# Feed-forward of a hybrid decoder layer: seven block products in the place of eight (2x2x2 blocks)

## The chip, the core and the metric

The kernel runs on one NeuronCore of a Trainium2 chip. The metric is device time in microseconds (us) of one execution. The engines that matter here are TensorE (PE in the profile; PEld is its weight load), VectorE (DVE), ScalarE (ACT), GpSimd (POOL) and SyncE (SP), whose queue issues the loads from memory. [...]

## What is computed

One layer for 544 tokens: 512 of a prompt and 8 x 4 of running sequences. The change touches the two products of the feed-forward alone:

```python
def layer_norm(x, g, b):
...
    mix = (jax.nn.sigmoid(g_a) * y_a + jax.nn.sigmoid(g_b) * y_b) @ w_out
    x1 = layer_norm(DN_ALPHA * x + mix, ln1_g, ln1_b)
    ff = jnp.square(jax.nn.relu(x1 @ w_ff1)) @ w_ff2
    ple = jax.nn.sigmoid(x1 @ w_ple_gate) * (p @ w_ple_proj)
    y = layer_norm(DN_ALPHA * x1 + ff + ple, ln2_g, ln2_b)
```

`x1` is 544 x 1024, `w_ff1` 1024 x 4096 and `w_ff2` 4096 x 1024, all in float32.

## The kernel before

Activations lie with the channels on the 128 partitions and the 544 tokens along a row, so a weight tile is 128 x 128 and a column tile of a product is 128 output channels by 544 tokens. The tokens are worked on in two runs of columns, 256 and 288 (`HALVES`), which lie in two PSUM banks of one buffer.

Every product of float32 numbers is made of three: each operand is split into a high part, rounded by a ScalarE copy to the type that TensorE reads (`hi`, `x1h`, `hid_0h`), and a low part, the VectorE difference of the operand and its high part (`lo`, `x1l`, `hid_0l`); the three passes of `mm` are high weight by high activation, high by low, and low by high. Each weight tile thus costs three passes over 544 columns.

Weights come as a stream of chunks (128 x 1024 numbers, 512 KB). `stream` loads a chunk into one of three `raw` buffers by SP's queue, ScalarE makes `hi`, VectorE makes `lo`, a few chunks ahead of TensorE. `pair` takes two column tiles of a product: two chunks for 1024 input channels, two PSUM buffers of the ring `mm` (three buffers of two banks each, `mm_psum`), and an evacuation function for each column tile when its sum is complete. While one tile is evacuated, TensorE works on the next in another buffer.

The feed-forward goes in quarters of the 4096 hidden channels, in the order of `ff_order`: stage (1, q) makes quarter q of the hidden layer, where ScalarE applies ReLU and the square and VectorE makes the low part (`evac_ff1`), and stage (2, q) multiplies that quarter by its part of `w_ff2` and VectorE adds the result from PSUM to the eight accumulators `acc` (`evac_ff2`). The last stage, (2, 3), runs with `by_halves`: all column tiles for the first run of tokens and then for the second, so that the second layer norm can begin (`between3`). Before the feed-forward stand the first layer norm and the per-layer gate (`evac_ple`), which set `x1` and the first value of `acc`.

The order in which an engine's instructions stand is set by `fill` and the class `Clocks`: work beside the products waits in sequences (`put`), and is issued where the planner's estimate of the engine's time falls behind its estimate for TensorE, or when its due chunk comes (`need`). All instructions go through one helper, so they all have one line in the profile (line 137) and are told apart by the tiles they read and write.

Of the kernel before, what the change touches and what calls it, by code (L numbers as in the profile page):

```python
# [9 lines left out]
F32 = mybir.dt.float32  # L10
# [5 lines left out]
P = 128  # L16
# [7 lines left out]
# the 544 token columns lie in two PSUM banks, as 256 + 288 neighbouring columns  # L24
# [3 lines left out]
SLOTS = 71  # L28
# [12 lines left out]
LN1_PRIO = 0.1  # L41
STREAM_PRIO = 0.15
# [19 lines left out]

def tname(x):
    return x.tensor.name
# [9 lines left out]
class Clocks:  # L74
    """estimates of when each engine comes to its work, from which the order of issue follows"""
# [35 lines left out]
    def op(self, e, name, out, args, kw):  # L111
# [4 lines left out]
        if e == "D":  # L116
# [25 lines left out]
def tile_hybrid_step(ctx: ExitStack, tc: tile.TileContext, I, O):  # L142
# [35 lines left out]
    # ---------------------------------------------------------------- constants  # L178
# [11 lines left out]
    # TensorE has its full clock only after a stretch of work: begin that while the first loads are under way  # L190
# [5 lines left out]
    # ---------------------------------------------------------------- weight stream  # L196
# [15 lines left out]

    raws, his, splits, held, fast, stacked = {}, {}, {}, set(), set(), set()
# [11 lines left out]
    def parts(j, tag):  # L225
        """a chunk's split weights: one buffer, or two of the activations' for a chunk that is held for long"""
# [34 lines left out]
    def split_first(a, b):  # L261
        """columns a to b of the first chunk, which comes in pieces"""
# [16 lines left out]
    def stream(e, i):  # L279
        """the next load, high or low part of a weight that engine e may take up beside chunk i"""  # L280
# [70 lines left out]
    def fill():  # L351
        horizon = clocks.t["T"] + LEAD
        moved = True
        while moved:
            moved = False
            for e in "DSVGT":
                while clocks.t[e] < horizon:
                    now = clocks.t[e]
                    it = stream(e, state["next"] - 1)
# [23 lines left out]
    # ---------------------------------------------------------------- products  # L383
# [13 lines left out]
    def pair(acts, mt0, evac, nkt=None):  # L397
        """two 128-column tiles of a product; its chunks come next in the stream"""
# [13 lines left out]
    def by_halves(acts, mt0, nmt, evac, between=None):  # L412
        """column tiles, all of the first token half before the second"""
# [21 lines left out]
    def split_later(prio, src, name, done_, due, *deps):  # L435
        """the two parts of an activation as a sequence of its own"""
# [18 lines left out]
    # ---------------------------------------------------------------- stream order  # L455
# [32 lines left out]
    ff_order = [(1, 0), (1, 1), (2, 0), (1, 2), (2, 1), (1, 3), (2, 2), (2, 3)]  # L488
    for kind, q in ff_order:
        if kind == 1:  # L490
            plan(I["w_ff1"][0], D, 1024 * q, 4)
        else:
            for p in range(4):
                for r in range(2):
                    w_spec(I["w_ff2"][0], 1024 * q + 512 * r, 4, 256 * p, 256)
    held.update(range(len(specs) - 4, len(specs)))

    # ---------------------------------------------------------------- x, feature-major
# [27 lines left out]
    # ---------------------------------------------------------------- parameters and states  # L526
# [37 lines left out]
    def param_math():  # L564
        # softplus(-lam) = max(-lam, 0) + 2 atanh(e / (2 + e)), e = exp(-|lam|)
# [19 lines left out]
        # c2 * r is half of -log(a)  # L585
# [3 lines left out]
    # ---------------------------------------------------------------- layer norms  # L589
    class Norm:  # L590
        """mean and variance over the 1024 channels of eight feature-major tiles, per token half"""
# [52 lines left out]
        def put(self, h, prio, due, after, *deps):  # L644
            """queue the steps up to 1 / deviation, and then after()"""
# [101 lines left out]
    # ---------------------------------------------------------------- branch b  # L747
# [519 lines left out]
```

## Time and profile before

| what | value |
|---|---|
| median of 3 runs | 1005.63 us (1005.08 to 1007.27) |
| span of the profiled execution, first to last instruction | 1004.8 us |
| mean granted TensorE clock, whole span | 0.984 |
| loads and stores | 97.87 MB, mean 97 GB/s |

The profile gives the profiled execution by its span; that execution has no separate time, and the median of the runs stands 0.8 us above the span. Busy time is the time in which an engine had an instruction in flight; records of neighbouring instructions can overlap, so the step from one start to the next is what an engine is occupied with one, and the duration is how long until its result is there. "x24" in a row of the timeline merges 24 equal instructions.

### The profile page before, as it was taken

Reading aid. Unit: us, or ns where it says so; the run is one execution under the profiler, and the core shown is the slowest. Engines: PE = TensorE matmul, PEld = TensorE weight load, DVE = VectorE, ACT = ScalarE, POOL = GpSimd, SP = SyncE. Lnnn points to the kernel's source line nnn. Section 1 sums busy time; section 2 is a strip of 40 time slices with the busy share of each in tenths; the row PEclk is TensorE's granted clock in tenths of the full one; section 3 lists DMA queues with packets and bytes.
Section 4 is the critical chain, followed back from the end, with each engine's and each line's share of the span. In section 5 each row is a group of like instructions: output and inputs, shape, how many; then the busy total and the mean of one; then the engine's idle time right before and its main releaser. Section 6 shows DMA issues by size and latency. Waiting matters only on the chain.

```text
span 1004.8 us, 17739 instructions
## 1 busy us (share of the span) xinstructions
PE 964.2 (96%) x7560; PEld 959.4 (95%) x7560; DVE 646.2 (64%) x939; ACT 413.1 (41%) x600; POOL 179.6 (18%) x173
## 2 busy tenths in 40 slices
PE   8999979989889997999999999999999999999995
PEld 8999979989889997999999999999999999999995
DVE  5698889897899999794468952323322222233447
ACT  6432428643467321563225834455114511541301
POOL 0342765455332700001200000000000000000002
PEclk9999989999899998999999999999999999999998
DMA  8333324332332222326251402222232332222402
GB/s 291 93 95 103 107 65 155 104 100 61 88 117 73 64 78 91 107 84 197 84 169 43 125 24 84 85 84 85 87 99 73 97 108 84 85 84 85 125 29 84
DMA packets 89279, 97.87 MB, mean 97 GB/s; under 512 B 4208, under 2 KB 82416, under 8 KB 89200
## 3 DMA queue, kind: packets, MB, share of 16 engines
q1 hardware_dynamic: 89200, 96.74, 31.1%
q8 instruction: 59, 0.97, 0.4%
q14 instruction: 20, 0.16, 0.1%
HBM read 89.71 MB, written 3.81 MB: 93 GB/s over the span
## 4 chain that ended last, share of the span: by engine, by line
PE 72%; DVE 12%; POOL 7%; ACT 5%; issue 3%; DMA 1%; SPq 0%; DVEq 0%; ACTq 0%; POOLq 0%
PE ps L137 55%; PE psq L137 14%; DVE ca L137 5%; DVE lo L137 2%; POOL prod L137 2%; POOL cbs L137 2%; POOL ctx_b L137 1%; PE pps L137 1%; ACT th L137 1%; PE rg L137 1%; ACT L137 1%; ACT hi L137 1%; ACT aa L137 1%; DVE s L137 1%; DVE th L137 1%
## 5 line engine op out<-in xcount | busy, mean ns | idle before, releaser
L137 ACT ACTIVATE hi<-raw 128x1024 fp32r<-128x1024 f32 (+4 forms) x177 | 167.7, 957 | 284.1 <-PE ps L137 217.2
L137 DVE TENSOR_TENSOR lo<-raw,hi 128x1024 fp32r<-128x1024 f32 (+3 forms) x173 | 194.4, 1148 | 13.2 <-ACT hi L137 13.0
L137 DVE SCALAR_TENSOR_TENSOR ca<-u,par_a,ca 128x482 f32<-128x482 f32 (+29 forms) x240 | 179.6, 806 | 1.3 <-ACT ca L137 0.9
L137 PE MATMUL ps<-x1l,hi 128*128 128x288 f32 x616 | 128.3, 290 | 0.6 <-DVE x1l L137 0.6
L137 PE MATMUL ps<-x1h,hi 128*128 128x288 f32 x616 | 127.6, 289 | 0.6 <-ACT x1h L137 0.6
L137 PE MATMUL ps<-x1h,lo 128*128 128x288 f32 x616 | 127.6, 288 | 0.0
L137 PEld LDWEIGHTS ps<-x1h,hi 128*128 128x128 f32 x616 | 94.8, 189 | 0.8 <-ACT x1h L137 0.8
L137 PEld LDWEIGHTS ps<-x1l,hi 128*128 128x128 f32 x616 | 94.6, 189 | 0.8 <-DVE x1l L137 0.8
L137 PEld LDWEIGHTS ps<-x1h,lo 128*128 128x128 f32 x616 | 94.9, 189 | 0.0
L137 POOL TENSOR_TENSOR y<-y,rows_g 128x512 f32<-128x512 f32 x2 | 3.1, 1547 | 461.1 <-ACT y L137 461.1
L137 DVE TENSOR_TENSOR acc<-acc,ps 128x544 f32<-128x544 f32 x24 | 17.3, 722 | 93.8 <-PE ps L137 93.8
L137 ACT ACTIVATE ff<-ps 128x544 f32<-128x544 f32 x32 | 20.0, 624 | 51.2 <-PE ps L137 51.2
L137 POOL TENSOR_TENSOR prod<-ctx_a,par_a 128x248 f32<-128x248 f32 x32 | 36.9, 1206 | 0.0
L137 PE MATMUL psq<-x1l,hi 128*128 128x288 f32 (+1 forms) x128 | 36.9, 288 | 0.0
L137 PE MATMUL psq<-x1h,lo 128*128 128x288 f32 (+1 forms) x128 | 36.8, 288 | 0.0
L137 PE MATMUL psq<-x1h,hi 128*128 128x288 f32 (+1 forms) x128 | 36.8, 287 | 0.0
L137 PE MATMUL ps<-x0h,hi 128*128 128x288 f32 x104 | 23.2, 306 | 10.5 <-ACT gate L137 9.0
L137 PEld LDWEIGHTS ps<-x0h,hi 128*128 128x128 f32 x104 | 16.7, 198 | 11.7 <-ACT gate L137 9.7
L137 PE MATMUL ps<-x0h,lo 128*128 128x288 f32 x104 | 22.3, 297 | 5.3 <-DVE lo L137 5.3
L137 ACT ACT_TABLE_LOAD x20 | 25.7, 1283 | 1.4 <-PEq L1257 0.7
L137 POOL COPY ctx_b<-bx 128x32 f32<-128x32 f32 x10 | 21.2, 2125 | 26.6 <-ACT bx L137 26.6
L137 POOL TENSOR_TENSOR sa<-sa,sb 128x544 f32<-128x544 f32 x6 | 10.9, 1812 | 77.3 <-DVE sa L137 77.3
(616 smaller groups left out, 2647.7 us busy)
## 6 DMA issues: line engine op xcount, KB each, us to landing
raw<-in_w_ff_dram SPq DMA_DIRECT2D x64, 512.0 KB, 4.2
raw<-in_w_in_dram SPq DMA_DIRECT2D x51, 512.0 KB, 3.6
xr<-in_x_dram SPq DMA_DIRECT2D x16, 272.0 KB, 5.3
raw<-in_w_proj_b_dram SPq DMA_DIRECT2D x8, 512.0 KB, 3.4
raw<-in_w_proj_a_dram SPq DMA_DIRECT2D x8, 512.0 KB, 4.1
raw<-in_w_out_dram SPq DMA_DIRECT2D x8, 512.0 KB, 3.5
raw<-in_w_ple_gate_dram SPq DMA_DIRECT2D x8, 512.0 KB, 3.9
out_dram<-y SPq DMA_DIRECT2D x8, 256.0 KB, 2.0
```

Source lines behind the costliest of these rows:

```text
L137: return fn(out, *args, **kw)
```

## The change

Both products of the feed-forward are cut into blocks of 256 x 256 weights and of 256 channels by 544 tokens. A block product is a 2 x 2 by 2 x 2 product of 128 x 128 weight tiles (A11, A12, A21, A22) and of activation pieces of 128 channels by 272 tokens (B11, B12, B21, B22), and it is made with seven products of pieces instead of eight. The seven products take the weights A11, S3, S2, A22, S1, A12 and S4 in this order (numbered 1, 7, 6, 4, 5, 2, 3), where S1 = A21 + A22, S3 = A11 + A21, S2 = S3 + A22 and S4 = S2 + A12 are formed by VectorE from the loaded blocks before they are split (`SUMS_BY_DMA = False`), and the activations B11, t3, t2, t4, t1, B21 and B22, where t1 to t4 are differences of the four pieces, formed by VectorE as well: once for `x1` (`plan_x_forms`) and once for each block of the hidden layer (`make_hid`). A "panel" is the seven products for 256 output channels. The four results of a panel are combined from partial sums: alpha (products 1, 6, 5, 3, one after another on top of each other), delta (7, 4) and beta (2). Alpha and beta lie in the two banks of one `mm` buffer, delta in a bank of the ring `misc`. Since alpha goes on growing, each of its intermediate values is read by ScalarE or VectorE before the next product is added to it.

There are 16 panels of 256 hidden channels for `w_ff1`, of which the first is made plainly with eight products (`ff1_four`, which needs no t1 to t4), and for `w_ff2` four groups of three hidden blocks, each with four panels (`ff2_seven`), while the last four hidden blocks are multiplied plainly by halves (`ff2_halves`), as the last quarter was before. The weights are laid out on the host by blocks; a load brings 128 x 512 (w_ff1) or 128 x 384 numbers (w_ff2), 256 or 192 KB, and two of them share a `raw` buffer. A loaded or summed block is a unit with its own place in `raw`, `hi` and `lo`. `SLOTS`, the number of activation buffers, goes from 71 to 72.

```diff
+FORM_AHEAD = {"D": 7, "G": 6, "V": 4, "S": 5}
+HALF = T // 2
+SUMS_BY_DMA = False
...
-    ff_order = [(1, 0), (1, 1), (2, 0), (1, 2), (2, 1), (1, 3), (2, 2), (2, 3)]
...
+    SEVEN = ("A11", "S3", "S2", "A22", "S1", "A12", "S4")
+    FOUR = ("A11", "A12", "A21", "A22")
...
+        else:
+            lo(us["A11"])
+            total(us["S3"], us["S1"], us["A11"])
+            total(us["S2"], us["S3"], us["A22"])
+            lo(us["S3"])
+            total(us["S1"], us["S1"], us["A22"])
+            lo(us["S2"])
+            lo(us["A22"]), lo(us["S1"])
+            total(us["S4"], us["S2"], us["A12"])
+            lo(us["A12"]), lo(us["S4"])
...
+    GROUPS = ((0, 3), (3, 3), (6, 3), (9, 3), (12, 4))
+    stages = []
+    for g, upto in enumerate((4, 7, 10, 14, 16)):
+        start = (0, 4, 7, 10, 14)[g]
+        stages += [(1, p) for p in range(start, upto)] + [(2, g)]
...
+        def t13():
+            a.extend(act(f"xt{q}_{i}") for i in range(2))
+            V.tensor_sub(half(a[0], 0), b11, b12)
+            V.tensor_sub(half(a[0], 1), b22, b12)
+
+        def t24():
+            V.scalar_tensor_tensor(half(a[1], 0), half(a[0], 0), -1.0, b22, op0=OP.mult, op1=OP.subtract)
+            V.scalar_tensor_tensor(half(a[1], 1), half(a[1], 0), -1.0, b21, op0=OP.mult, op1=OP.subtract)
...
+    def mm3(ps, u, k, a, start, stop, more):
+        w = slice(k * P, k * P + P)
+        for pi, (ww, aa) in enumerate(((u.hi, a[0]), (u.hi, a[1]), (u.lo, a[0]))):
+            TE.matmul(ps, ww[:, w], aa, start=start and pi == 0, stop=stop and pi == 2,
+                      skip_group_check=more)
+
+    def seven(fs, name, after):
+
+        ab, d = mm_psum(name), misc_psum(name + "d")
+        al, be, de = ab[:, :HALF], ab[:, 512:512 + HALF], d[:, :HALF]
+        for nm, ps, start, b in ((1, al, True, "B11"), (7, de, True, "t3"), (6, al, False, "t2"), (4, de, False, "t4"),
+                                 (5, al, False, "t1"), (2, be, True, "B21"), (3, al, False, "B22")):
+            u = take()
+            for k, f in enumerate(fs):
+                mm3(ps, u, k, f()[b], start and k == 0, k == len(fs) - 1, not start)
+                fill()
+            release(u)
+            after(nm, ps)
+            fill()
...
+            elif nm == 4:
+                b["Y"], b["Z"] = act(f"fy{p}"), act(f"fz{p}")
+                c21 = half(b["Z"], 0) if plain else half(b["Y"], 1)
+                V.scalar_tensor_tensor(c21, ps, -1.0, half(b["W"], 0), op0=OP.mult, op1=OP.subtract)
+            elif nm == 5:
+                c22 = half(b["Z"], 1 if plain else 0)
+                V.scalar_tensor_tensor(c22, ps, -1.0, half(b["X"], 1), op0=OP.mult, op1=OP.subtract)
+            elif nm == 2:
+                V.tensor_add(half(b["Y"], 0), ps, half(b["X"], 0))
...
+    def ff2_seven(g):
+        q0, nq = GROUPS[g]
+        for mp in range(4):
+            c = [[half(acc[2 * mp + i], l) for l in range(2)] for i in range(2)]
+
+            def after(nm, ps):
+                out, op = {1: (c[0][0], V.tensor_add), 7: (c[1][1], V.tensor_sub), 6: (c[1][0], V.tensor_sub),
+                           4: (c[1][0], V.tensor_sub), 5: (c[1][1], V.tensor_sub), 2: (c[0][0], V.tensor_add),
+                           3: (c[0][1], V.tensor_add)}[nm]
+                op(out, out, ps)
+            seven([lambda q=q: hid_forms[q] for q in range(q0, q0 + nq)], f"g{g}_{mp}", after)
...
-    for kind, q in ff_order:
+    for kind, n in stages:
         if kind == 1:
-            e = evac_ff1(q)
-            for p in range(4):
-                pair(x1, 2 * p, e)
-        elif q < 3:
-            for p in range(4):
-                pair(hid[q], 2 * p, evac_ff2)
-            hid[q] = None
+            (ff1_seven if n else ff1_four)(n)
+            if n == 15:
+                x1 = x_forms = None
+        elif n < 4:
+            ff2_seven(n)
         else:
-            by_halves(hid[q], 0, 8, evac_ff2, between3)
+            ff2_halves()
```

The order of the instructions moves on every engine. First place, TensorE within a panel of `w_ff2`, before: column tiles of a stage (2, q); `ps` is the PSUM buffer of the tile, `hid` the hidden layer, and two runs of columns follow each other for every pair of operands.

```order
L137 MATMUL ps_0_8888<-hid_4h,hi_8784 128x288
L137 MATMUL ps_0_8888<-hid_4h,hi_8784 128x256
L137 MATMUL ps_0_8888<-hid_4l,hi_8784 128x288
L137 MATMUL ps_0_8888<-hid_4l,hi_8784 128x256
L137 MATMUL ps_0_8888<-hid_4h,lo_8834 128x288
L137 MATMUL ps_0_8888<-hid_4h,lo_8834 128x256
```

The changed kernel at the end of product 5 (weights S1, activation t1, called hh0B), through product 2 (A12, B21, hh0A) to the beginning of product 3 (S4, B22). `g_2_7716` is the buffer that holds both alpha and beta of the third panel of the first group; the words in brackets name the semaphores that an instruction waits for (DVE is VectorE's, Activation ScalarE's).

```order
L149 MATMUL g_2_7716<-hl2B,fhi_7696 128x272
L149 MATMUL g_2_7716<-hh2B,flo_7697 128x272
L149 MATMUL g_2_7716<-hh0A,fhi_7725 128x272 [waits DVE_49,Activation_49]
L149 MATMUL g_2_7716<-hl0A,fhi_7725 128x272
L149 MATMUL g_2_7716<-hh0A,flo_7726 128x272
L149 MATMUL g_2_7716<-hh1A,fhi_7725 128x272
L149 MATMUL g_2_7716<-hl1A,fhi_7725 128x272
L149 MATMUL g_2_7716<-hh1A,flo_7726 128x272
L149 MATMUL g_2_7716<-hh2A,fhi_7725 128x272
L149 MATMUL g_2_7716<-hl2A,fhi_7725 128x272
L149 MATMUL g_2_7716<-hh2A,flo_7726 128x272
L149 MATMUL g_2_7716<-hh0B,fhi_7725 128x272 [waits DVE_49,Activation_49]
```

A sum that was made of one uninterrupted run into its own buffer is now made of products that each begin with a wait for VectorE. In the built program the first of the two values waited for is the one that VectorE reaches with its sum after product 5 (`acc_6263<-acc_6263,g_2_7716`), and the second the one after product 2; beta and alpha are different banks, but one tile to the framework that sets the waits.

Second place, VectorE in the same stretch, before: `acc` is an accumulator, `lo` a low part of the weight stream.

```order
L137 TENSOR_TENSOR acc_6260<-acc_6260,ps_0_8888 128x544
L137 TENSOR_TENSOR acc_6261<-acc_6261,ps_1_8889 128x544
L137 TENSOR_TENSOR lo_9004<-raw_8836,hi_8944 128x1024
L137 TENSOR_TENSOR lo_9058<-raw_8894,hi_9002 128x1024
L137 TENSOR_TENSOR acc_6262<-acc_6262,ps_0_9000 128x544
```

The changed kernel from product 6 of that panel to product 1 of the next: `fraw` are weight blocks and sums (a row `fraw<-fraw` is a sum), `flo` low parts, `g_2d` is delta.

```order
L149 TENSOR_TENSOR acc_6263<-acc_6263,g_2_7716 128x272
L149 TENSOR_TENSOR acc_6263<-acc_6263,g_2d 128x272
L149 TENSOR_TENSOR flo_7769<-fraw_7732,fhi_7768 128x384
L149 TENSOR_TENSOR fraw_7776<-fraw_7732 128x384
L149 TENSOR_TENSOR acc_6263<-acc_6263,g_2_7716 128x272
L149 TENSOR_TENSOR fraw_7790<-fraw_7776 128x384
L149 TENSOR_TENSOR flo_7769<-fraw_7776,fhi_7768 128x384
L149 TENSOR_TENSOR acc_6262<-acc_6262,g_2_7716 128x272 x2
L149 TENSOR_TENSOR fraw_7732<-fraw_7732,fraw_7776 128x384
L149 TENSOR_TENSOR flo_7799<-fraw_7790,fhi_7798 128x384
L149 TENSOR_TENSOR flo_7799<-fraw_7776,fhi_7798 128x384
L149 TENSOR_TENSOR flo_7827<-fraw_7732,fhi_7826 128x384
```

Four instructions for two column tiles have become eighteen for the same two column tiles, and the seven that read PSUM stand between the others.

Third place, VectorE at the beginning of the feed-forward, before: from the last step of the gate stage on.

```order
L137 SCALAR_TENSOR_TENSOR acc_6265<-res_5886,acc_6265 128x256
L137 TENSOR_TENSOR lo_6844<-raw_6420,hi_6722 128x1024
L137 TENSOR_TENSOR lo_6898<-raw_6491,hi_6842 128x1024
L137 TENSOR_TENSOR hid_0l<-ff_0_6926,hid_0h 128x544
L137 TENSOR_TENSOR hid_1l<-ff_1_6957,hid_1h 128x544
```

The changed kernel from the same step on; `xt` are the differences t1 to t4 of `x1`.

```order
L149 SCALAR_TENSOR_TENSOR acc_6265<-res_5886,acc_6265 128x256
L149 TENSOR_TENSOR flo_6832<-fraw_6825,fhi_6831 128x512 x2
L149 TENSOR_TENSOR flo_6836<-fraw_6828,fhi_6835 128x512 x2
L149 TENSOR_TENSOR flo_6849<-fraw_6840,fhi_6848 128x512
L149 TENSOR_TENSOR xt_0_6861<-res_5634 128x272
L149 TENSOR_TENSOR xt_0_6861<-res_5662,res_5634 128x272
L149 TENSOR_TENSOR xt_0_6871<-res_5716 128x272
L149 TENSOR_TENSOR xt_0_6871<-res_5754,res_5716 128x272
L149 SCALAR_TENSOR_TENSOR xt_1_6862<-xt_0_6861,res_5662 128x272
```

The first low parts of `w_ff1` moved behind the last step of the gate stage (before, those of the first chunk stood ahead of it), and 24 instructions on `xt` stand between them and most of the second panel's low parts.

More of the change, by code (lines that the diff above doesn't have):

```diff
@@ L60 @@
 INF = float("inf")
+split_names = set()
 def tname(x):
-    return x.tensor.name
+    n = x.tensor.name
+    return n + "+" if n in split_names and x.offset % 1024 >= 512 else n
 def width(ap):
@@ L115, in op @@
                     + [self.ready.get(tname(a), 0.0) for a in ins])
-        if e == "D":
+        if name == "dma_start" and e == "G":
+            self.t["G"] = start + 1.0
+            self.dma = max(self.dma, start + 1.6) + width(out) * out.shape[0] * 4 / 180e3
+            end = self.dma + 1.2
+        elif e == "D":
             self.t["D"] = start + 0.47
@@ L279, in stream @@
     def stream(e, i):
+        if forms is not None and {"D": state["loaded"], "S": state["hi"], "V": state["lo"]}.get(e, INF) >= len(specs):
+            return forms.offer(e)
         more = 2 if i in fast else 0
@@ new lines, in tile_hybrid_step, with out_of, may_have @@
+    units, tasks = [], {e: deque() for e in "DGSV"}
+    raw_pairs, split_pairs = {}, {}
+    at = {"now": -1, "done": 0}
+    single = set()
+    def out_of(pairs, v, tag):
+        if tag == "raw":
+            return len(raws) + sum(1 for q in raw_pairs.values() if q.left)
+        return in_buffers(NCH) - in_buffers(state["done"]) + sum(1 for q in split_pairs.values() if q.left)
+    def may_have(kind, r):
+        pairs, bufs = (raw_pairs, RAW_BUFS) if kind == "raw" else (split_pairs, SPLIT_BUFS)
+        v = r // 2
+        if v in pairs:
+            return True
+        if v and v - 1 not in pairs:
+            return False
+        return out_of(pairs, v, kind) < bufs
@@ new lines, in tile_hybrid_step, with __init__, have_raw, raw_read @@
+    class Slot:
+        def __init__(self):
+            self.left = 2
+    def have_raw(u):
+        v = u.r // 2
+        if v not in raw_pairs:
+            s = raw_pairs[v] = Slot()
+            s.pair = Pair("raw", f"fraw{v}", F32)
+        u.raw = raw_pairs[v].pair.piece(u.r % 2, u.n)
+    def raw_read(u):
+        u.left -= 1
+        if not u.left:
+            u.raw = None
+            s = raw_pairs[u.r // 2]
+            s.left -= 1
+            if not s.left:
+                s.pair = None
@@ new lines, in have_split, with release @@
+    def have_split(u):
+        if u.kept:
+            u.hi, u.lo = (act(f"k{u.i}{c}", F32R)[:, :u.n] for c in "hl")
+            return
+        v = u.s // 2
+        if v not in split_pairs:
+            s = split_pairs[v] = Slot()
+            s.left -= v in single
+            s.hi, s.lo = Pair("hi", f"fhi{v}", F32R), Pair("lo", f"flo{v}", F32R)
+        s = split_pairs[v]
+        u.hi, u.lo = (q.piece(u.s % 2, u.n) for q in (s.hi, s.lo))
+    def release(u):
+        u.hi = u.lo = None
+        if not u.kept:
+            s = split_pairs[u.s // 2]
+            s.left -= 1
+            if not s.left:
+                s.hi = s.lo = None
@@ new lines, in tile_hybrid_step, with offer, run, take @@
+    add_units.r = add_units.s = 0
+    class forms:
+        @staticmethod
+        def offer(e):
+            if not tasks.get(e):
+                return None
+            i, gate, when, fn = tasks[e][0]
+            if i > at["now"] + FORM_AHEAD[e] or not gate():
+                return None
+            def run():
+                tasks[e].popleft()
+                fn()
+            return when(), run
+    def take():
+        at["now"] += 1
+        u = units[at["now"]]
+        need(NCH + u.i)
+        while not getattr(u, "lo_done", False):
+            moved = False
+            for e in "DGSV":
+                while tasks[e] and tasks[e][0][0] <= u.i + 3 and tasks[e][0][1]():
+                    tasks[e].popleft()[3]()
+                    moved = True
+                    if u.lo_done:
+                        break
+            assert moved, (u.i, u.name, {e: (t[0][0], t[0][1]()) for e, t in tasks.items() if t})
+        fill()
+        return u
@@ new lines, in ff2_halves @@
+    def ff2_halves():
+        us = []
+        for h in range(2):
+            for m in range(8):
+                if h == 0:
+                    us += [[take(), take()]]
+                ps = mm_psum(f"psq{h}_{m}")
+                for q in range(4):
+                    for j in range(2):
+                        u, (hi, lo) = us[m][j], hid[12 + q][j]
+                        for pi, (ww, aa) in enumerate(((u.hi, hi), (u.hi, lo), (u.lo, hi))):
+                            TE.matmul(tokh(ps, h), ww[:, q * P:q * P + P], cols(aa, h),
+                                      start=q == 0 and j == 0 and pi == 0, stop=q == 3 and j == 1 and pi == 2)
+                        fill()
+                a = cols(acc[m], h)
+                V.tensor_add(a, a, tokh(ps, h))
+                if h == 1:
+                    for u in us[m]:
+                        release(u)
+                between3(h, m)
```

270 lines of the change are left out of this document (246 added, 24 removed).

## The prediction

> **What bounds the kernel now.** I read the page's busy times and slices first, then the feed-forward by windows, then single rows of the timeline there.
>
> ```profile
> span 1004.8 us, 17739 instructions
> PE 964.2 (96%) x7560; PEld 959.4 (95%) x7560; DVE 646.2 (64%) x939; ACT 413.1 (41%) x600; POOL 179.6 (18%) x173
> PE   8999979989889997999999999999999999999995
> DVE  5698889897899999794468952323322222233447
> ```
>
> TensorE bounds the whole span. VectorE is the second engine, but its slices differ: 8 or 9 tenths up to 600 us, 2 to 4 in the feed-forward (slices 24 to 39). A window of the feed-forward:
>
> ```profile
> core 0: us, PE busy (x) PEld busy (x) DVE busy (x) ACT busy (x) POOL busy (x), PEclk, DMA share, GB/s
> 650.00:700.00 50.00, 50.00 (x402) 50.00 (x401) 15.13 (x17) 25.18 (x35) 0.00 (x0) 1.00 0.28 85
> ```
>
> TensorE does not pause for a moment, at full clock; VectorE has 35 of 50 us free, ScalarE 25, the DMA queues 72%. So fewer matmuls shorten this part by exactly their own time, as long as TensorE does not pause. Their price comes from two rows of ScalarE, the high part of the first tile of two successive pairs of column tiles. Between them TensorE works off one pair: 2 tiles x 8 weight tiles x 3 passes x 2 runs = 96 matmuls:
>
> ```profile
> 651.01 0.66 ACT L137 ACTIVATE hid_6h<-ff 128x544 fp32r<-128x544 f32 x1
> 663.02 0.66 ACT L137 ACTIVATE hid_0h<-ff 128x544 fp32r<-128x544 f32 x1
> ```
>
> 12.01 us / 96 = **0.1251 us** for the mean of 288 and 256 columns, which is 272, the new width.
>
> **The matmuls.** The feed-forward has 3,072 now (2 products x 256 weight tiles x 3 passes x 2 runs). After: the plain panel 96 and 15 panels of 84 (w_ff1), 16 panels of 63 and the plain quarter's 384 (w_ff2), 2,748. 324 x 0.1251 = **-40.5 us**.
>
> **The waits this adds.** The sums now grow in place, and the shown order makes product 2 wait until VectorE has read product 5, and product 3 until it has read product 2. Nothing lies between, so TensorE stands through a whole round trip, twice in each of 31 panels, 62 times; behind the waiting matmul stands all of TensorE's queue. No row has this round trip whole, but its pieces:
>
> ```profile
> 966.34 0.29 PE L137 MATMUL psq<-hid_7h,lo 128*128 128x288 f32 x1
> 966.47 0.28 PE L137 MATMUL psq<-hid_0h,hi 128*128 128x256 f32 x1
> 966.67 0.45 DVE L137 TENSOR_TENSOR acc<-acc,psq 128x288 f32<-128x288 f32 x1 [2.72 <-PE psq L137]
> 189.82 0.62 ACT L137 ACTIVATE gate<-ps 128x544 f32<-128x544 f32 x1
> 190.50 0.52 PE L137 MATMUL ps<-x0h,hi 128*128 128x288 f32 x2 [1.49 <-ACT gate L137]
> 190.86 0.41 PE L137 MATMUL ps<-x0l,hi 128*128 128x288 f32 x2
> ```
>
> The last matmul's slot ends at 966.47, where the next begins, and an idle VectorE begins to read 0.20 later and takes 0.45 (0.43 at 272, between this and the 0.42 of 256 columns). From the end of an evacuation (190.44) to TensorE's first matmul are 0.06, and its first pair takes 0.36 in place of the usual 0.25, 0.11 more. Together 0.20 + 0.43 + 0.06 + 0.11 = **0.80 us**. Bounds: 0.43, if only the evacuation itself counts, and 1.0, if the hand-over back costs TensorE as much again. I take 0.80, each piece having its row. 62 x 0.80 = **+49.6 us**: already more than the matmuls saved.
>
> [...]
>
> **VectorE's queue.** What stands ahead of the seven reads decides when they start. From start to start VectorE needs:
>
> ```profile
> 948.00 2.49 DVE L137 TENSOR_TENSOR lo<-raw,hi 128x512 fp32r<-128x512 f32 x4
> 407.02 0.42 DVE L137 TENSOR_TENSOR lnasl<-sum_a,lnash 128x256 fp32r<-128x256 f32 x1
> 407.36 1.54 DVE L137 TENSOR_TENSOR ca<-ca,lnamu 128x288 f32<-128x288 f32 x4
> 408.81 0.45 DVE L137 TENSOR_TENSOR lnav<-lnav,lnasq 128x288 f32<-128x288 f32 x1
> 11.81 0.72 DVE L137 TENSOR_TENSOR x4l<-xr,x4h 128x544 fp32r<-128x544 f32 x1
> 12.44 0.72 DVE L137 TENSOR_TENSOR x5l<-xr,x5h 128x544 fp32r<-128x544 f32 x1
> 588.00 0.43 DVE L137 TENSOR_TENSOR acc<-acc,pp 128x256 f32<-128x256 f32 x1 [1.94 <-ACT acc L137]
> 588.46 0.42 DVE L137 SCALAR_TENSOR_TENSOR acc<-res,acc 128x256 f32<-128x256 f32 x1
> ```
>
> 0.34 for 256, 0.36 for 288 ((408.81 - 407.36) / 4), 0.60 for 512 ((2.49 - 0.685) / 3, its mean being 685 ns as the last instruction's), 0.63 for 544; so 0.35 for 272 and, on the line between, 0.47 for 384. An instruction on the result just made starts 0.12 later than its own step (0.46 for 0.34).
>
> A w_ff2 panel asks of VectorE 11 x 0.47 + 7 x 0.35 = 7.6 us, less than TensorE's 63 x 0.1251 + 1.60 = 9.48; so it is not the bound by sum, but by order. One steady panel, product 1 ending at 0, each product 1.126: ahead of its read stand S1', lo S2, lo A22, lo S1 (the order's last rows, since the read of product 3), so it starts at 1.3, not 0.2, and product 6 at 1.9, not 1.13. Product 6 ends 3.0, is read at 3.4; product 4 ends 4.15, product 5 at 5.27. Then VectorE reads 4 (4.35), makes a low part and a sum (4.70, 5.17), and reads 5 at 5.64 in place of 5.47. Product 2 ends 7.36, product 3 at 9.28, the next panel's product 1 at **10.4**. That is 0.92 above 9.48; x 16 = **+14.7 us**. Bounds: 0, if low parts slip into gaps, and 2 x 0.47 per exposed read, 16 x 1.9 = +30.
>
> A w_ff1 panel takes 84 x 0.1251 + 1.60 = 12.1. VectorE's 11 x 0.60, three reads, and a hidden block's forms (two differences, two combined at 0.35 to 0.47, three low parts at 0.63 and one at 0.35, 3.8 us) are 11.5, also below. But in the eight panels beside which forms are made, five of these (two sums or low parts at 0.60, three of forms near 0.63, 3.1 us) stand between the reads of product 5 and 2, where product 2 covers 1.5 and the bubble 0.4: 1.2 late, 8 x 1.2 = **+9.6**. The three groups whose last forms fall on the first w_ff2 panel add 2 each, **+6**. Bounds of both: 0 and twice that, if ScalarE's squares, for which the next difference waits, come late too.
>
> **The start.** The rows of before, where the gate ends:
>
> ```profile
> 605.48 0.42 DVE L137 SCALAR_TENSOR_TENSOR acc<-res,acc 128x256 f32<-128x256 f32 x1
> 605.82 2.35 DVE L137 TENSOR_TENSOR lo<-raw,hi 128x1024 fp32r<-128x1024 f32 x2
> ```
>
> Before, the first chunk's low part was made earlier (it stood ahead in the order). After, the first 512-column low parts come from 605.82 on; the plain panel's first product reaches its third pass long before: I take 2.0, between 0.6 (one low part) and 2.5 (four). The 24 instructions on x1 (4 x (2 x 0.35 + 2 x 0.47 + 2 x 0.63) = 11.6 us), the low parts of two panels (5 + 11 times 0.60 = 9.6) must pass beside one plain panel of 12.0 and the part of the next before t3: 3.5 late. Together **+5.5**, bounds 1 and 10.
>
> **At no cost.** Loads: the bytes per us are those of before within a tenth, at a DMA share of 0.28. ScalarE makes seven high parts of a panel's weights in place of four, and those of t1 to t4:
>
> ```profile
> 946.63 1.15 ACT L137 ACTIVATE hi<-raw 128x512 fp32r<-128x512 f32 x2 [3.50 <-DMA raw<-in_w_ff_dram]
> ```
>
> At 0.58 each (1.15 / 2) 7 are 4.0 us, and eight passes over 544 columns (ReLU, square, high parts) at the 0.66 of the rows above 5.3: 9.3 us of a w_ff1 panel's 12.1, so beside TensorE; if it came last there instead of VectorE, the waits would be those bounded above. The end is as before by halves; if its cover went, one low part at a tile's start, 0.6 us.
>
> **Sum:** -40.5 + 49.6 + 14.7 + 9.6 + 6 + 5.5 = +44.9 on the span of 1004.8: 1049.7. The runs' median stands 0.8 above it: **1050.5 us**.
>
> **Rivals.** *Bubbles alone*: VectorE's low parts fit into the gaps, as its sums of 7.6 in 9.5 and 11.5 in 12.1 would allow. -40.5 + 49.6 + 5.5 = +14.6, **1020**. Against it stands the order, which is fixed when the program is built.
> [...]
> *The clock falls*: TensorE now stops every few us. The rows on the clock:
>
> ```profile
> 185.00:190.00 5.00, 4.01 (x33) 1.00 0.34 110
> 190.00:195.00 5.00, 4.50 (x35) 1.00 0.51 146
> 215.00:220.00 5.00, 2.22 (x9) 0.73 0.36 107
> ```
>
> A fifth of idle time kept 1.00; over half gave 0.73. The new idle share is about 1.6 to 2.5 of 10.4, near the first. If the clock still fell to 0.94 over some 430 us of feed-forward, 430 x (1 / 0.94 - 1) = 27 us more than forecast: **1078**. [...]
> *No change*: bubbles of 0.56 and a queue on time, **1006**.
>
> **How the numbers follow.** Chances: forecast 0.72, its own range 1030 to 1066 (62 x 0.15 us of the bubble and half of the queue's terms to either side); bubbles alone 0.14; clock 0.05; faster 0.06; no change 0.03. From bubbles alone with 2 us below it to the forecast's upper end, 1018 to 1066, leaves out 0.14 and the forecast's tails, about 0.2. A measurement of this kernel tells apart some 0.2%, 2 us: faster 0.06, same 0.03, slower 0.91.
>
> **What would show it.** Right: 2,748 matmuls in the feed-forward at 0.125 us each; two idle times of about 0.8 us in each panel, released by VectorE's reads; panels of 10.4 (w_ff2) and 12.1 to 13.3 us (w_ff1); a clock of 1.00. Wrong: idle times at product 6 or none at 2 and 3; panels of 9.5 (bubbles alone); TensorE without pauses (the wait is not what the order says); windows with a clock below 0.97; a gap of over 10 us at the start, which would mean loads or x1's forms.

## The result, and the profile after

The changed kernel takes 1072.03 us (median of 4 runs, 1069.68 to 1072.98) against 1005.43 us before: 1.066 times as long, 95% interval 1.064 to 1.069. The profiled execution was the shortest of the four, 1069.68 us with a span of 1067.9, 63.1 above the span of before.

The page of the changed kernel, the lines that answer to those of before:

```profile
span 1067.9 us, 18165 instructions
PE 955.0 (89%) x7236; PEld 930.0 (87%) x7236; DVE 853.8 (80%) x1461; ACT 497.7 (47%) x875; POOL 174.9 (16%) x173
PE   9999989998899979999999987788788788778895
DVE  4789999988999998945787688778878777777547
PEclk9999989999899999999999999999999999989998
PE 46%; DVE 31%; ACT 7%; POOL 6%; DMA 5%; issue 4%; SPq 0%; DVEq 0%; ACTq 0%; POOLq 0%
```

In the kernel before, the chain that ended last (the work followed back from the last instruction, at each step to what released it) was made up so:

```profile
PE 72%; DVE 12%; POOL 7%; ACT 5%; issue 3%; DMA 1%; SPq 0%; DVEq 0%; ACTq 0%; POOLq 0%
```

324 matmuls are gone, but TensorE's slices in the feed-forward fell from 9 to 7 and 8, VectorE's rose from 2 to 4 to mostly 7 and 8, and VectorE's share of the chain that ended last from 12 to 31%. A window of the feed-forward (columns as before):

```profile
700.00:750.00 50.00, 41.64 (x313) 39.45 (x312) 39.02 (x77) 29.51 (x64) 0.00 (x0) 1.00 0.27 77
```

Neither engine is full: TensorE stands for 8.4 of 50 us and VectorE for 11. They wait for each other. A steady panel of w_ff2 shows how, first TensorE's matmuls ahead of which it waited (in brackets how long, and for whom), from product 6 of one panel to product 6 of the next:

```profile
687.35 0.36 PE L149 MATMUL g<-hh0C,fhi 128*128 128x272 f32 x1 [0.58 <-DVE acc L149]
691.89 0.36 PE L149 MATMUL g<-hh0A,fhi 128*128 128x272 f32 x1 [0.86 <-DVE acc L149]
693.88 0.37 PE L149 MATMUL g<-hh0B,fhi 128*128 128x272 f32 x1 [0.62 <-DVE acc L149]
698.09 0.36 PE L149 MATMUL g<-hh0C,fhi 128*128 128x272 f32 x1 [0.59 <-DVE acc L149]
```

and VectorE in the same stretch:

```profile
687.46 0.55 DVE L149 TENSOR_TENSOR fraw<-fraw,fraw 128x384 f32<-128x384 f32 x1
687.93 1.23 DVE L149 TENSOR_TENSOR flo<-fraw,fhi 128x384 fp32r<-128x384 f32 x2
689.09 0.43 DVE L149 TENSOR_TENSOR acc<-acc,g 128x272 f32<-128x272 f32 x1
689.87 0.44 DVE L149 TENSOR_TENSOR acc<-acc,g_2d 128x272 f32<-128x272 f32 x1 [0.36 <-PE g_2d L149]
690.37 0.56 DVE L149 TENSOR_TENSOR flo<-fraw,fhi 128x384 fp32r<-128x384 f32 x1
690.84 0.55 DVE L149 TENSOR_TENSOR fraw<-fraw 128x384 f32<-128x384 f32 x1
691.31 0.43 DVE L149 TENSOR_TENSOR acc<-acc,g 128x272 f32<-128x272 f32 x1
691.66 0.55 DVE L149 TENSOR_TENSOR fraw<-fraw 128x384 f32<-128x384 f32 x1
692.13 0.55 DVE L149 TENSOR_TENSOR flo<-fraw,fhi 128x384 fp32r<-128x384 f32 x1
693.29 0.44 DVE L149 TENSOR_TENSOR acc<-acc,g 128x272 f32<-128x272 f32 x1 [0.61 <-PE g L149]
```

One panel takes 698.09 - 687.35 = 10.74 us. Three of its seven products begin with a wait for a read. The read of product 2 (693.29) starts at once, VectorE has been idle for 0.61, and TensorE still waits 0.62: that is the bare round trip. The read of product 5 (691.31) had a low part and a sum ahead of it, and there the wait is 0.86.

TensorE's rows divide the feed-forward into its stages (from the first matmul of one to that of the next). "w_ff1" and "w_ff2" are all panels up to the last stage:

| stretch, us | before | after | forecast |
|---|---|---|---|
| first instruction to first matmul of w_ff1 | 604.40 | 601.75 | 604.4 |
| w_ff1, 16 panels | 192.2 | 216.3 | 208.6 |
| w_ff2, all but the last quarter | 144.4 | 184.3 | 172.4 |
| last quarter, to the last transposes | 51.6 | 53.4 | 51.6 |

The first row differs by up to 6 us among the profiles below, and no experiment edits anything ahead of the gate's end; so the experiments are read by these stretches as well as by their medians.

### The profile page after: what moved, and what is told of

Same layout as the page of the kernel before. It is cut to its first block, busy times and chain, and to the rows that moved or that the text cites. A ratio compares the mean times of both kernels' runs of the same rounds, so it can differ in the third digit from the quotient of the medians.

```text
span 1067.9 us, 18165 instructions
## 1 busy us (share of the span) xinstructions
PE 955.0 (89%) x7236; PEld 930.0 (87%) x7236; DVE 853.8 (80%) x1461; ACT 497.7 (47%) x875; POOL 174.9 (16%) x173
## 4 chain that ended last, share of the span: by engine, by line
PE 46%; DVE 31%; ACT 7%; POOL 6%; DMA 5%; issue 4%; SPq 0%; DVEq 0%; ACTq 0%; POOLq 0%
PE ps L149 18%; PE psq L149 13%; DVE ca L149 9%; PE f L149 6%; PE g L149 6%; DMA fraw<-in_w_ff_dram 4%; DVE flo L149 4%; DVE lo L149 3%; DVE fraw L149 3%; DVE acc L149 2%; ACT fhi L149 2%; POOL prod L149 2%; ACT fy L149 1%; POOL cbs L149 1%; PE pps L149 1%
## 5 line engine op out<-in xcount | busy, mean ns | idle before, releaser
L149 ACT ACTIVATE fhi<-fraw 128x512 fp32r<-128x512 f32 (+1 forms) x229 | 125.4, 574 | 153.2 <-DVE fraw L149 133.7
L149 DVE TENSOR_TENSOR flo<-fraw,fhi 128x512 fp32r<-128x512 f32 (+1 forms) x229 | 136.9, 620 | 30.4 <-ACT fhi L149 28.7
L149 ACT ACTIVATE hi<-raw 128x1024 fp32r<-128x1024 f32 (+3 forms) x109 | 100.0, 928 | 112.5 <-PE ps L149 56.5
L149 DVE TENSOR_TENSOR lo<-raw,hi 128x1024 fp32r<-128x1024 f32 (+3 forms) x105 | 121.0, 1166 | 12.8 <-ACT hi L149 12.8
L149 PE MATMUL f<-x1h,fhi 128*128 128x272 f32 x212 | 61.7, 303 | 31.5 <-DVE fy L149 17.1
L149 POOL TENSOR_TENSOR y<-y,rows_g 128x512 f32<-128x512 f32 x2 | 3.1, 1554 | 528.0 <-ACT y L149 528.0
L149 DVE TENSOR_TENSOR acc<-acc,g 128x272 f32<-128x272 f32 x80 | 34.7, 434 | 35.6 <-PE g L149 35.5
L149 PE MATMUL f<-x1h,flo 128*128 128x272 f32 x212 | 58.6, 289 | 0.2 <-DVE flo L149 0.2
L149 PE MATMUL f<-x1l,fhi 128*128 128x272 f32 x212 | 58.4, 288 | 0.0
L149 DVE TENSOR_TENSOR fraw<-fraw,fraw 128x384 f32<-128x384 f32 (+1 forms) x76 | 46.6, 614 | 0.9 <-DMA fraw<-in_w_ff_dram 0.9
L149 PEld LDWEIGHTS f<-x1h,flo 128*128 128x128 f32 x212 | 38.9, 188 | 0.5 <-DVE flo L149 0.5
L149 PEld LDWEIGHTS f<-x1l,fhi 128*128 128x128 f32 x212 | 39.0, 189 | 0.0
```

Source lines behind the costliest of these rows:

```text
L149: return fn(out, *args, **kw)
```

## The experiments

Theory: the time comes from waits that the new dependencies add, of two separate kinds: the two bare round trips (products 2 and 3), and reads that stand behind weight work in VectorE's queue. The main rival: VectorE has become the bound by its amount of work, and the waits only show where it catches up. All medians are set against the kernel before in the same runs (1005.4 to 1006.6 us). An edit changes more than its own lines: the planner follows buffers and costs, so it issues a part of VectorE's instructions in another order as well. With own buffers that is at least 132 of VectorE's last 701 instructions, with the filled waits at least 56.

| run | median, us | ratio to before, 95% interval | w_ff1 | w_ff2 |
|---|---|---|---|---|
| changed kernel | 1072.0 | 1.064 to 1.069 | 216.3 | 184.3 |
| own_buffers | 1019.5 | 1.012 to 1.016 | 189.6 | 153.6 |
| no_sums | 1044.4 | 1.037 to 1.040 | 206.4 | 163.9 |
| own_no_sums | 983.0 | 0.976 to 0.979 | 173.8 | 136.1 |
| sums_on_gpsimd | 1113.2 | 1.100 to 1.113 | 248.8 | 193.6 |
| own_and_gpsimd | 1043.9 | 1.036 to 1.040 | 201.3 | 171.3 |
| own_and_dma | 1127.4 | 1.119 to 1.122 | 238.5 | 215.4 |
| filled_waits | 1069.3 | 1.061 to 1.064 | 218.6 | 178.3 |
| forms_later | 1068.4 | 1.060 to 1.064 | 220.3 | 176.6 |
| own_forms_later | 1014.3 | 1.004 to 1.009 | 176.5 | 161.5 |
| w_ff1_alone | 1033.9 | 1.026 to 1.029 | 216.4 | 144.3 |
| own_w_ff1_alone | 1010.2 | 1.003 to 1.005 | 189.6 | 144.3 |
| own_w_ff1_ordered | 990.7 | 0.983 to 0.986 | 174.9 | 144.3 |

**The round trips.** `own_buffers` takes them away by two lines:

```diff
-        ab, d = mm_psum(name), misc_psum(name + "d")
-        al, be, de = ab[:, :HALF], ab[:, 512:512 + HALF], d[:, :HALF]
+        a_, b_, d = mm_psum(name), mm_psum(name + "b"), misc_psum(name + "d")
+        al, be, de = a_[:, :HALF], b_[:, :HALF], d[:, :HALF]
```

> Alpha and beta get a ring buffer of their own each, so that product 2 no longer waits for VectorE's read of product 5, and product 3 has a whole product between it and that read; nothing else is changed. Theory (two exposed round trips in each of 31 panels, 0.79 us each in the steady panels of the changed kernel, are the largest single term): the idle times ahead of products 2 and 3 go, 62 x 0.8 = 50 us less, 1012 to 1024 us. Rival (VectorE's queue is the bound and the round trips only give it time to catch up): the idle time moves to other products, mainly to 6 and 5, and less than 25 us are gained, above 1047 us.

Measured: 52.5 us less, as the theory has it. TensorE at products 5, 2, 3 and the next product 1 of a panel, first and last matmul of each:

```profile
828.78 0.36 PE L149 MATMUL g<-hh6B,fhi 128*128 128x272 f32 x1
829.88 0.29 PE L149 MATMUL g<-hh8B,flo 128*128 128x272 f32 x1
830.00 0.28 PE L149 MATMUL g_2b<-hh6A,fhi 128*128 128x272 f32 x1
831.00 0.29 PE L149 MATMUL g_2b<-hh8A,flo 128*128 128x272 f32 x1
831.12 0.29 PE L149 MATMUL g<-hh6B,fhi 128*128 128x272 f32 x1
832.12 0.29 PE L149 MATMUL g<-hh8B,flo 128*128 128x272 f32 x1
832.25 0.29 PE L149 MATMUL g<-hh6A,fhi 128*128 128x272 f32 x1
```

From one matmul's start to the next are 0.12 to 0.13 us, also where one product follows another: no wait is left in this piece. One buffer for two independent sums cost more than all the matmuls that the scheme saves (40.5 us). The 52.5 us hold what the new order on VectorE brought, too; the round trip alone is priced below, in a pair of runs.

**The sums in VectorE's queue.** `no_sums` leaves the four sums out, so it does not compute the layer; each of their places is loaded with one of the blocks:

```diff
-            first = PARTS[nm][0] if nm[0] == "A" else {"S1": "A21", "S3": "A11"}.get(nm) if by_dma else \
-                {"S1": "A21"}.get(nm)
+            first = PARTS[nm][0] if nm[0] == "A" else {"S1": "A21", "S3": "A11", "S2": "A22", "S4": "A12"}[nm]
...
-            total(us["S3"], us["S1"], us["A11"])
-            total(us["S2"], us["S3"], us["A22"])
...
```

> The sums S1 to S4 are left out: each of the four places is loaded with one of its blocks, seven loads for a panel in place of four, so VectorE has seven weight instructions a panel in place of eleven and no engine makes the sums. Theory: as with the sums on GpSimd, without what GpSimd might cost, 1035 to 1045 us. Rival (the queue's order and not its length delays the reads): within 10 us of the changed kernel, above 1060 us.

27.7 us less, inside the theory's range. This is the price of the sums with all that hangs on them: ScalarE's high parts and VectorE's low parts of a sum no longer wait for it either. With both edits:

> A buffer each for alpha and beta, and the sums left out (their four places are loaded with one block each, seven loads in place of four). Theory (both terms add): 1019.5 - 28 = 989 to 995 us. Rival (with the round trips gone VectorE is the bound, so its sums count by their whole time): up to 15 x 2.4 + 16 x 1.9 = 66 us less than with them, below 980 us.

983.0 us, 89.1 less than the changed kernel: 6 below the theory's range, 3 above the rival's mark. The two alone add up to 52.5 + 27.7 = 80.2, so they are separate terms in the main, and 9 us come only with both: without the round trips the sums weigh 36.5 us in place of 27.7, which fits a VectorE that then has less time to catch up; no run shows that reason by itself. The run also shows the scheme's size: with the sums left out it is 23 us, 2.3%, faster than the kernel before.

This pair of runs prices the round trip best, since without the sums VectorE is on time. A steady panel of w_ff2 in `no_sums`, from product 1 to product 1, with its only two waits:

```profile
924.65 0.28 PE L149 MATMUL g<-hh9A,fhi 128*128 128x272 f32 x1
931.07 0.36 PE L149 MATMUL g<-hh9A,fhi 128*128 128x272 f32 x1 [0.62 <-DVE acc L149]
933.06 0.36 PE L149 MATMUL g<-hh9B,fhi 128*128 128x272 f32 x1 [0.62 <-DVE acc L149]
934.25 0.28 PE L149 MATMUL g<-hh9A,fhi 128*128 128x272 f32 x1
```

It takes 9.60 us; with own buffers as well it takes 7.90 (669.17 to 677.07) and has no wait, so a bare round trip costs 1.70 / 2 = 0.85 us. That is more than the 0.62 in brackets, which begin only where the last matmul's record ends, 0.29 us after its start, while matmuls without a wait start every 0.125 us.

**Other engines for the sums.** GpSimd in place of VectorE (one word in the sum and its queue):

```diff
-                V.tensor_add(u.raw, a.raw, b.raw)
+                G.tensor_add(u.raw, a.raw, b.raw)
```

> The four weight sums of a panel go from VectorE to GpSimd, which is idle in the feed-forward; the round trips stay. Theory (what stands ahead of VectorE's reads costs the rest): the steady w_ff2 panel goes from 10.74 to about 9.7 us and the w_ff1 panel from 13.3 to about 12.3, 16 x 1.0 + 15 x 1.0 = 31 us less, about 1041 us. Rival (GpSimd needs about 1.5 us for a sum of 512 columns, by its rows of the layer norm's end, and its sums come too late or slow VectorE's own instructions): 1065 us or more.

41 us more, and the rival says why. VectorE's low parts and reads, in the groups by form:

```profile
L149 DVE TENSOR_TENSOR flo<-fraw,fhi 128x512 fp32r<-128x512 f32 x117 | 103.9, 904 | 36.8 <-ACT fhi L149 36.7
L149 DVE TENSOR_TENSOR acc<-acc,g 128x272 f32<-128x272 f32 x80 | 34.7, 434 | 50.6 <-PE g L149 50.6
```

and in the changed kernel:

```profile
L149 DVE TENSOR_TENSOR flo<-fraw,fhi 128x512 fp32r<-128x512 f32 x117 | 77.6, 685 | 22.1 <-ACT fhi L149 21.4
L149 DVE TENSOR_TENSOR acc<-acc,g 128x272 f32<-128x272 f32 x80 | 34.7, 434 | 35.6 <-PE g L149 35.5
```

A low part, which reads and writes SBUF alone, grew from 685 to 904 ns; a read with one operand in PSUM stayed at 434. An addition of 128x512 takes GpSimd 1.55 us (`y<-y,rows_g` on the page of the changed kernel, 1554 ns; a sum of that size takes VectorE 0.68), and the low part and the next sum wait for it. The clock adds to this: it stood at half speed for 92 us of this run's feed-forward (in the changed kernel for 17; mean granted clock of the span 0.942 against 0.978), at most 46 us lost. How much of the 41 us the slower instructions cost directly and how much the falls of the clock behind TensorE's longer waits, this run does not separate.

> Both edits together: a buffer each for alpha and beta, and the sums on GpSimd. Theory (both terms are separate and add up): 50 + 31 us less than the changed kernel, about 990 us, which would be less than the kernel before. Rival (the two are the same time seen twice): no less than the better of the two alone, above 1010 us.

1043.9, above the rival's mark, since the second edit is a loss by itself: the round trips come back more than whole (69 us less than with GpSimd's sums and one buffer), but the sums cost 24 us more on GpSimd than on VectorE (31 us at half clock, 7 with own buffers alone; mean granted clock of the span 0.967 and 0.976). The third way uses the switch that the change brings along, `SUMS_BY_DMA = True`, for two of the four:

> A buffer each for alpha and beta, and two of the four sums (S1 and S3) made by loads that add to what is there, on GpSimd's queue, so that VectorE makes two. Theory (half of VectorE's sums): half of the 28 us that leaving all of them out brought, 1003 to 1009 us, and low parts as short as without (686 ns for 512 columns). [...]

108 us worse than with own buffers, so the theory falls. The low parts are as short as hoped (687 ns), but the two sums that VectorE still makes wait for the loads, 35.6 us in the larger form, of 512 columns, and 39.9 in the smaller one (the larger in the groups by form; idle time and its cause last):

```profile
L149 DVE TENSOR_TENSOR fraw<-fraw,fraw 128x512 f32<-128x512 f32 x30 | 20.6, 688 | 35.6 <-DMA fraw<-in_w_ff_dram 35.6
```

An adding load takes, by the page, a median of 4.4 us from issue to landing:

```profile
fraw<-in_w_ff_dram POOLq DMA_DIRECT2D x30, 256.0 KB, 4.4
```

It adds to what an earlier load has brought, so that a sum comes after two loads in a row. The clock was at half speed for 96 us of this feed-forward (mean of the span 0.941), so at most 48 of the 108 us are its own.

**The clock.** In the changed kernel's profile the granted clock halves in four places of the feed-forward; single microseconds of one of them, and the first and last of the next (TensorE's busy time, clock, DMA share, GB/s):

```profile
667.00:668.00 1.00, 0.72 (x6) 1.00 0.32 109
668.00:669.00 1.00, 0.00 (x0) 1.00 0.56 144
669.00:670.00 1.00, 0.31 (x1) 0.65 0.17 59
670.00:671.00 1.00, 1.00 (x6) 0.50 0.00 0
...
672.00:673.00 1.00, 1.00 (x7) 0.65 0.00 0
...
839.00:840.00 1.00, 0.00 (x0) 0.98 0.31 109
843.00:844.00 1.00, 1.00 (x8) 0.81 0.00 0
```

A clock of 0.65 over a microsecond is 0.7 us at half speed: the fall lasts from 669.3 to 672.7, 3.4 us, and the next from 839.96 to 843.4. The others begin at 621.5 (3.4 us) and at 938.95 (6.8). Together 17 us at half speed, at most 8.5 us lost. `filled_waits` puts work into the idle time:

```diff
+            if nm in (2, 3):
+                for _ in range(4):
+                    TE.matmul(de, u.hi[:, :P], fs[0]()["B11"][0], start=True, stop=True)
```

> The changed kernel with four more matmuls ahead of product 2 and of product 3 in each panel, into the bank of delta, which VectorE has read by then and which product 7 of a later panel begins anew; their result is not used. They need 4 x 0.125 = 0.5 us and stand where TensorE now waits 0.8. Theory (TensorE's clock fell to 0.50 for 3.4 us or twice that in four places of the feed-forward because of the idle share ahead of them, some 8 us lost): with less idle time at least half of these places go, 1063 to 1069 us, and the clock is 1.00 there. Rival (the long waits at the first two panels of a group cause them, not the round trips): no change, 1070 to 1075. If the round trip were not idle time at all: 62 x 0.5 = 31 us more.

No fall is left in its feed-forward (mean granted clock of the span 0.983, in the changed kernel 0.978); the place of one of them:

```profile
834.00:840.00 6.00, 5.20 (x36) 1.00 0.28 91
840.00:846.00 6.00, 4.61 (x35) 1.00 0.13 42
```

The median is 2.7 us lower, just outside the theory's range: the three groups of w_ff2 that had a fall are 2.2, 1.2 and 2.6 us shorter, the one that had none is 0.1 longer, and w_ff1 gave 2.4 back, for a reason that no run here separates (added matmuls that are not hidden, or the other order on VectorE). 62 times half a microsecond of matmuls, 31 us, made the kernel no longer, which shows once more that the round trip is idle time of TensorE.

**The forms.** The other long waits stand in the first two panels of a w_ff2 group. VectorE in the first panel, ahead of the read of product 2 (669.11):

```profile
665.97 1.49 DVE L149 TENSOR_TENSOR flo<-fraw,fhi 128x384 fp32r<-128x384 f32 x3
667.38 0.72 DVE L149 TENSOR_TENSOR hl3A<-fy,hh3A 128x544 fp32r<-128x544 f32 x1
668.01 0.55 DVE L149 TENSOR_TENSOR fraw<-fraw 128x384 f32<-128x384 f32 x1
668.48 0.71 DVE L149 TENSOR_TENSOR hl3C<-hc,hh3C 128x544 fp32r<-128x544 f32 x1
669.11 0.43 DVE L149 TENSOR_TENSOR acc<-acc,g 128x272 f32<-128x272 f32 x1
```

Product 2's last matmul began at 667.44. The low parts of block 3, which is needed a group later, hold its read up until 669.11, and TensorE waits 1.97. `forms_later` puts them behind the weight stream:

```diff
-        put(0.1, steps, due)
+        put(0.2, steps, due)
```

> The changed kernel with the forms of the hidden blocks (their squares, differences and low parts) behind the weight stream in the order of priority, not ahead of it. Theory (the forms of a panel that is needed only a group later stand ahead of reads and low parts in the first two panels of a w_ff2 group, which take 12.7 and 12.0 us in place of 10.7): 8 to 13 us less, 1059 to 1064. Rival (they must be made somewhere, and then come due all at once ahead of the group that needs them): within 4 us of the changed kernel, or slower.

3.7 us less, so the rival: w_ff2 gained 7.7 us and w_ff1 gave 4.0 back. With own buffers:

> A buffer each for alpha and beta, and the forms of the hidden blocks behind the weight stream in the order of priority. Theory (VectorE's total work bounds the panels now, so its order matters little): within 4 us of 1019.5. Rival (the order is what makes the low parts late): 8 us less or more, below 1012.

5.2 us less, between the two, and hardly clear of this kernel's own spread (1009.0 to 1016.0): w_ff1 gained 13.1 and w_ff2 lost 7.8. So the order matters for each stage, and moves the time from one to the other. The forms have to be made, and VectorE has little room for them; a window of `own_buffers` (TensorE, its weight loads, VectorE 47.5 of 50 us):

```profile
650.00:700.00 50.00, 44.87 (x341) 43.03 (x341) 47.49 (x103) 25.91 (x54) 0.00 (x0) 1.00 0.31 89
```

**A version that is faster.** Seven products should pay where VectorE has little beside the weights. `own_w_ff1_alone` makes them in w_ff1 only, without any forms of the hidden layer:

```diff
-            plain = p >= 12
+            plain = True
...
-            ff2_seven(n)
+            ff2_four(n)
```

> A buffer each for alpha and beta, and seven products only in w_ff1; all of w_ff2 is made plainly with eight (column tiles of 128 channels, one read by VectorE each), so that the hidden layer needs high and low parts alone, none of the forms t1 to t4. Theory (both terms as measured, and VectorE off the path once the forms are gone: its 8.9 us in a w_ff1 panel against TensorE's 10.5): 15 panels at 10.6, as the last two of the run with own buffers took (21.1 / 2), in place of 12.0, 15 x 1.4 = 21 us less than before, 2 to 4 us lost at the start: 985 to 992 us, faster than the kernel before. Rival (four sums and seven low parts a panel still make VectorE late, as in the panels of 11.8 to 12.2 us with own buffers): no gain over eight products, 1000 us or more.

1010.2, 0.4% slower than before and 18 us above the forecast's upper end. Leaving out the forms did not shorten w_ff1: 189.6 us, as with them. The three panels of the second group took 32.0 us, as forecast, but in the last panel of a group ScalarE has the hidden layer's squares ahead of the high parts that TensorE needs, and behind the last panel of all nothing is left to do while its hidden block is made:

```profile
791.38 0.39 PE L149 MATMUL f<-xt0h,fhi 128*128 128x272 f32 x1 [1.61 <-ACT fhi L149]
946.97 0.61 PE L149 MATMUL psq<-hp15h,fhi 128*128 128x288 f32 x1 [2.69 <-ACT hp15h L149]
```

The round trips are priced once more by the same kernel with one buffer:

> The same with alpha and beta in one buffer, as in the changed kernel. Theory: two round trips of 0.8 us in each of 15 panels, 24 us above the run with own buffers, 1009 to 1016 us, so slower than the kernel before. Rival (with a VectorE that has time to spare the round trips are short): less than 12 us above.

1033.9, 23.7 us more for 30 round trips, 0.79 each. By the stretch of w_ff1 it is 26.8 us, 0.89 each; the run with own buffers gave some 4 us back in its last quarter (57.7 against 53.3 us). Then the two waits on ScalarE are removed by order:

```diff
-    for g, upto in enumerate((4, 7, 10, 14, 16)):
-        start = (0, 4, 7, 10, 14)[g]
+    for g, upto in enumerate((4, 7, 10, 16, 16)):
+        start = (0, 4, 7, 10, 16)[g]
...
-            put(0.1, steps + [("S", lambda t=t: square(t)), ("S", high), ("V", low)], due)
+            put(0.2, steps + [("S", lambda t=t: square(t)), ("S", high), ("V", low)], due)
```

> As the run with own buffers and seven products in w_ff1 alone, with two changes of order: all 16 panels of w_ff1 stand ahead of the last plain group of three hidden blocks (as the last quarters stood in the kernel before), and the squares and high parts of the hidden layer come behind the weight stream in priority. Theory (what that run lost are waits of 1.6 to 2.7 us on ScalarE at the last w_ff1 panel of a group and ahead of the last hidden block, with three or four falls of the clock behind them, and a tail of 57.7 in place of 51.6 us): 6 us less at the end, 6 to 14 in w_ff1, 988 to 999 us, faster than the kernel before. Rival (the waits come from sums that VectorE makes too late, whatever ScalarE's order): within 5 us of 1010.

990.7 us, 1.6% faster than the kernel before and inside the forecast: w_ff1 is 14.7 us shorter, the last quarter 6.0, so the rival falls. The two edits were not run apart. The order shortened w_ff1, and not the missing forms alone: with the forms made, but behind the weight stream, it took 176.5 us (`own_forms_later`, where a part of their work went into w_ff2), here 174.9. TensorE has 180 matmuls less than there, by the page, and is as full again, by a window:

```profile
PE 944.2 (95%) x7380; PEld 936.8 (95%) x7380; DVE 748.9 (76%) x1197; ACT 459.1 (46%) x791; POOL 178.6 (18%) x173
```

```profile
700.00:750.00 50.00, 50.00 (x401) 50.00 (x400) 29.77 (x53) 25.11 (x55) 0.00 (x0) 1.00 0.34 107
```

## Why the prediction was right in kind and too small

The forecast of 1050.5 (1018 to 1066) had the right sign and named the waits that came; the measured 1072.0 lies 6 us beyond its upper end, with a loss half as large again as forecast. The step that failed is the price of VectorE's queue (14.7, 6 and 9.6, together 30.3 us), walked through one steady panel and carried over to nearly all, and beside it the clock, which was put at nothing. The two products came out 19.6 us longer than forecast; at most 8.5 of that are the clock's and some 3 the round trips' (62 times 0.85 in place of 0.80), so the queue's terms should have been 38 us or more.

- **The matmuls, -40.5.** Right: nothing in the trace contradicts it, and with own buffers a product of nine matmuls steps in 1.12 to 1.13 us.
- **The round trips, 62 x 0.80 = +49.6.** Right: 0.85 us from the steady panels without sums, 0.79 (by the medians) or 0.89 (by the stretch) from 30 of them, and 52.5 us from all. The rivals "faster" (a round trip below (40.5 - 5.5) / 62 = 0.56) and "no change" (one of 0.56) fall with this.
- **VectorE's queue in w_ff2, +14.7, and its first panels, +6: too small.** The steady panel was walked to 10.4 and took 10.74, waits in the places that were named (ahead of products 6, 2 and 3). But the walk was taken for all panels but four. The first panels of the four groups took 12.7 on average (forecast 12.4, and 10.4 in the last group) and the second ones 12.0, where 10.4 was forecast: forms of the next group's blocks, which the forecast had put beside w_ff1 and the first panel alone, and falls of the clock. w_ff2 is 11.9 us longer than forecast. In `filled_waits`, which has no falls, it is 6.0 us shorter (first panels 12.5, second ones 11.0), so about half of the 11.9 is the queue, and the rest came with the falls.
- **w_ff1, +9.6 in eight panels.** A panel with forms beside it took 13.36 (640.13 to 653.49, product 2 to product 2), as forecast (13.3). But the delay came in nearly all panels: the last two, which have no forms beside them, took 27.0 / 2 = 13.5 where 12.1 was forecast. w_ff1 is 7.7 us longer. What delays the panels without forms was not taken apart.
- **The start, +5.5.** The first four panels, with it, took 56.5; the terms make 12.0 + 3 x 12.1 + 2 x 1.2 + 5.5 = 56.2. The sum is right by luck: 3.4 us of this stretch ran at half clock, 1.7 us lost, which no term had. Nor does its part of 3.5 us follow from the numbers that stand with it (11.6 + 9.6 us of VectorE's work beside 12.0 us and product 1's 1.5 would leave 7.7); the waits there were 0.2 us at t3 and 1.8 at the low part of product 6.
- **The clock.** A row of 5 us in which a fifth was idle at a clock of 1.00 was taken as proof, and the rival of a clock of 0.94 throughout, the author's assumption, was priced at 27 us and put aside at 0.05. The mean idle share of a panel was the wrong measure: the falls follow single stretches with long waits, in which TensorE was busy for 1.46 to 1.72 of 3.4 us (last section). What happened lay between: up to 8.5 of the 19.6 us by which the two products came out longer, from falls in four places and not throughout.
- **The rest.** The span came out 18 us above the forecast; the other 3 are the median's distance from it, 4.1 us (0.8 before), since the profiled execution was the shortest.
- **The rival "bubbles alone", 1020,** is wrong for the changed kernel; it would need VectorE's queue to cost nothing, and `no_sums` shows 27.7 us that hang on the sums in it. Without the sums the steady panel takes 9.60 us, close to the 9.48 of this rival.

## What to carry to other kernels

When sums grow in place, count the waits that are fully exposed before counting the instructions saved: two independent sums in one PSUM buffer cost some 50 us here, and a second buffer, two changed lines, gave them back. An algorithm that trades matmuls for additions is worth what the adding engine has free in that very stage: with own buffers seven products lost in w_ff2 (153.6 against 144.4 us) and won in w_ff1 once the hidden layer's work stood behind the weights (176.5 with the forms and 174.9 without, against 192.2). A walk through one steady period must be repeated for the first and last periods of a stage, where work of the neighbouring stages stands in the queues.

## What the runs showed of the hardware

- The falls of the clock in the changed kernel's feed-forward begin at 621.5, 669.3, 839.96 and 938.95 and last 3.4, 3.4, 3.4 and 6.8 us, at 0.50. In the 3.4 us ahead of each TensorE was busy for 1.63, 1.53, 1.46 and 1.72 us, with the clock at 1.00. From 921.88 to 925.28 it was busy for 1.67 us, and the clock stayed at 1.00 in the 3.4 us behind; waits of 0.62 and 1.66 us that end at 752.82 and 755.85 brought no fall either (1.00 from 750 to 758). So TensorE's busy time ahead does not by itself tell where the clock falls here, and no run shows what decides it.
- With the four sums on GpSimd (`sums_on_gpsimd`), VectorE's low parts, which read and write SBUF alone, took longer than in the changed kernel: 904 ns in place of 685 at 128x512 and 701 in place of 552 at 128x384. Its reads with an operand in PSUM took 434 ns as before.
